# Channel mixers of a two-layer encoder: up and down projections in 2x2 blocks with seven block products, the down projection as a stage of its own with its input by way of DRAM

## The chip, the cores and the metric

The kernel runs on one core of one Trainium2 chip. The metric is the device time of one execution in microseconds. The core's engines work from queues of their own: TensorE (PE, with its weight load PEld), VectorE (DVE), ScalarE (ACT), GpSimd (POOL) and SyncE (SP), which issues most of the transfers between DRAM and on-chip memory.

## What is computed

An encoder of two layers on 1280 tokens: a prompt of 256 and a sample of 1024. Layer 0 mixes tokens by RWKV-7, layer 1 by neighbourhood attention. After each mixer follow its output projection, the residual and a squared-ReLU network of width 4096 on 1024 features, with the same weights for prompt and sample:

```
def _sq_relu_mlp(h, w_up, w_down):
    return jnp.square(jax.nn.relu(h @ w_up)) @ w_down
...
x = x + mixer(_rms_norm(x, norm_mix_g[layer])) @ w_o
x = x + _sq_relu_mlp(_rms_norm(x, norm_mlp_g[layer]), w_up[layer], w_down[layer])
```

(The last two lines are put in short; the mixers' own formulas play no part here.)

## The kernel before

Features lie on the 128 partitions, tokens along the free dimension. The tokens are three segments: s0 is the prompt (256), s1 and s2 are the halves of the sample (512 each). Every matmul operand is split into a high part (a cast to fp32r) and a low part (what the cast left), and every product is three matmuls, high by high, high by low, low by high (`mm3`, L95, issued at L97, L98 and L99). A weight block of 128x1024 is loaded by SP, cast by ACT (L91), and its low part is a subtraction on POOL (L92).

`channel_layer` (L1322) does all that follows a mixer. First comes the **output projection**: for 8 blocks m of output features and three segments, 8 feature blocks k times three matmuls into one PSUM tile `ps` (24 matmuls). DVE adds the tile to the residual stream `x` (L1382), ACT and POOL form sums of squares (L1213, L1214), and `split_x` cuts x, times the norm's gain, into the next operands `ah`, `al` (L1221 on ACT, L1222 on DVE). The root mean square is not applied here: since the squared ReLU is homogeneous of degree two, `scale` (L1388) multiplies the residual x by the mean square ms (L1395, DVE and POOL in turns), and at the very end x is multiplied by its reciprocal (L1399, L1432).

Then come the **up and down projections, interleaved** for 32 blocks f of 128 hidden features: `up(f, s)` (L1401) is 24 matmuls, a ReLU on ACT (L1408), the square on POOL (L1409), the cast on ACT (L1411) and the low part on DVE (L1412). `down([f - 1], s)` (L1418) has 8 output blocks of three matmuls, each added to x by DVE (L1430):

```
for f in range(2, NF - 1):
    for s in range(3):
        up(f, s)
        down([f - 1], s)
    if rest and f > 4:
        inverse(*rest.pop())
    wdown(f)
```

Hidden activations therefore never leave the chip. The last two f go through one `down`, which also scales x, stores it and, in layer 0, splits it for the next layer (L1432 to L1434), sums its squares and takes the token norms; ten `v_block`s (L494, 24 matmuls of 256 columns) of the attention's value projection follow. The order of the instructions on every engine is a scheduler's, except on PE in that last piece. Seven PSUM tiles take turns.

## Time and profile before

| | us |
|---|---|
| median of 3 runs (lowest, highest) | 4359.28 (4358.39, 4360.66) |
| profiled execution, its own time | 4355.5 |
| its span, from the first instruction to the last | 4353.7 |
| mean granted TensorE clock | 0.951 |
| layer 0: output projection to the last v_block | 1648.6 to 2707.1 |
| layer 1: output projection to the end | 3334.9 to 4353.7 |

Times in the rows of the trace are counted from the span's start. Rows by stage or by line give busy time, the number of instructions and, by line, the mean duration in ns; then the idle time of the engine just before them and what ended it. A matmul's recorded duration overlaps its neighbours', so the cost of a matmul on PE is the distance between two starts. PEclk is the granted clock as a share of full speed.

### The profile page before, as it was taken

To read this page: it belongs to the slowest core of one execution; us is meant where nothing else is said; L and a number is where in the kernel's file an instruction comes from. 1 tells how busy PE (TensorE), PEld (TensorE's weight loads), DVE (VectorE), ACT (ScalarE), POOL (GpSimd) and SP (SyncE) were. 2 spreads that over 40 slices of the span, in tenths; PEclk is the share of its full clock that TensorE was granted. 3 is DMA by queue.
4 is the path that set the end of the run, shared out by engine and by line. 5 is a ranking of instruction groups with operands and counts; after the bars stand their busy time and mean duration, and the time that the engine had idled before them with its cause. 6 is when DMAs were issued, how large, how long until landed. Compare 5 with 4: busy or idle time off the path is not lost.

```text
span 4353.7 us, 69827 instructions
## 1 busy us (share of the span) xinstructions
PE 4048.0 (93%) x25060; PEld 3369.9 (77%) x25060; DVE 2695.7 (62%) x5276; ACT 1782.1 (41%) x4705; POOL 1672.1 (38%) x1706
## 2 busy tenths in 40 slices
PE   7888989789999879999999998989998999999999
PEld 4664669778777768888888888977776888888888
DVE  7888874477778755755555556156656665555555
ACT  6764442477777763211111114255545311111111
POOL 5446663234444443422222224134435432222222
PEclk8996779899999989999999999999998999999999
DMA  3234455665666424111111113433334211111111
GB/s 119 82 107 171 162 172 166 153 159 144 158 153 153 112 84 157 49 39 38 36 39 39 39 35 118 147 67 74 76 81 147 77 39 39 35 39 35 39 39 59
DMA packets 484155, 400.27 MB, mean 92 GB/s; under 512 B 289152, under 2 KB 392480, under 8 KB 483808
## 3 DMA queue, kind: packets, MB, share of 16 engines
q1 hardware_dynamic: 447584, 328.56, 27.2%
q10 hardware_dynamic: 34416, 61.35, 3.9%
q0 software_dynamic: 1808, 5.90, 0.4%
q8 instruction: 197, 3.23, 0.3%
q14 instruction: 150, 1.23, 0.1%
HBM read 285.66 MB, written 121.24 MB: 93 GB/s over the span
## 4 chain that ended last, share of the span: by engine, by line
PE 66%; DVE 6%; ACT 5%; DMA 3%; issue 2%; POOL 2%; SPq 1%; ACTq 0%; DVEq 0%; POOLq 0%
PE ps L97 16%; PE ps L99 16%; PE ps L98 16%; PE w L1057 2%; PE us L1029 2%; PE kps L950 1%; PE aps L809 1%; PE vps L501 1%; PE vps L502 1%; PE vps L503 1%; PE us L1043 1%; PE op L1873 1%; PE w L1009 1%; ACT u L1038 1%; PE pt L1815 1%
## 5 line engine op out<-in xcount | busy, mean ns | idle before, releaser
L1430 DVE TENSOR_TENSOR x<-ps,x 128x256 f32<-128x256 f32 x1488 | 814.7, 597 | 627.9 <-PE ps L99 627.7
L97 PE MATMUL ps<-ah,whi 128*128 128x512 f32 (+1 forms) x2304 | 844.2, 366 | 4.2 <-ACT whi L91 3.5
L98 PE MATMUL ps<-al,whi 128*128 128x512 f32 (+1 forms) x2304 | 824.6, 358 | 2.6 <-POOL al L1320 2.6
L99 PE MATMUL ps<-ah,wlo 128*128 128x512 f32 (+1 forms) x2304 | 824.7, 358 | 1.8 <-POOL wlo L92 1.5
L92 POOL TENSOR_TENSOR wlo<-raw,whi 128x1024 fp32r<-128x1024 f32 (+1 forms) x178 | 391.1, 2197 | 850.2 <-ACT whi L91 807.4
L97 PE MATMUL ps<-hh,whi 128*128 128x512 f32 (+1 forms) x1536 | 546.7, 356 | 13.9 <-DVE x L1430 13.9
L99 PE MATMUL ps<-hh,wlo 128*128 128x512 f32 (+1 forms) x1536 | 546.0, 355 | 0.0
L98 PE MATMUL ps<-hl,whi 128*128 128x512 f32 (+1 forms) x1536 | 545.3, 355 | 0.0
L97 PEld LDWEIGHTS ps<-ah,whi 128*128 128x128 f32 x2304 | 439.5, 191 | 78.9 <-issue 12.9
L99 PEld LDWEIGHTS ps<-ah,wlo 128*128 128x128 f32 x2304 | 438.7, 190 | 67.8 <-POOL wlo L92 2.7
L98 PEld LDWEIGHTS ps<-al,whi 128*128 128x128 f32 x2304 | 439.5, 191 | 63.0 <-POOL al L1320 3.0
L91 ACT CAST whi<-raw 128x1024 fp32r<-128x1024 f32 (+1 forms) x206 | 200.8, 975 | 699.2 <-PE ps L98 632.9
L1409 POOL TENSOR_TENSOR rl<-rl 128x512 f32<-128x512 f32 (+1 forms) x192 | 174.2, 907 | 500.5 <-PE ps L99 458.3
L97 PEld LDWEIGHTS ps<-hh,whi 128*128 128x128 f32 x1536 | 291.5, 190 | 57.5 <-DVE x L1430 16.9
L1408 ACT ACTIVATE rl<-ps 128x512 f32<-128x512 f32 (+1 forms) x192 | 100.8, 525 | 546.4 <-PE ps L99 546.4
L99 PEld LDWEIGHTS ps<-hh,wlo 128*128 128x128 f32 x1536 | 291.5, 190 | 41.1
L98 PEld LDWEIGHTS ps<-hl,whi 128*128 128x128 f32 x1536 | 291.3, 190 | 40.9
L1411 ACT CAST hh<-rl 128x512 fp32r<-128x512 f32 (+1 forms) x192 | 105.5, 549 | 320.9 <-POOL rl L1409 320.9
L1051 DVE SCALAR_TENSOR_TENSOR S<-us,dall,sd 64x64 f32<-64x64 f32 x512 | 145.0, 283 | 125.1 <-PE us L1043 113.3
L1013 POOL TENSOR_TENSOR sd<-S,dall 128x128 f32<-128x128 f32 x256 | 122.4, 479 | 256.0 <-DVE S L1051 173.2
L1412 DVE TENSOR_TENSOR hl<-rl,hh 128x512 fp32r<-128x512 f32 (+1 forms) x192 | 119.4, 622 | 151.6 <-ACT hh L1411 151.2
L1057 PE MATMUL w<-u,zb 128*128 128x128 f32 x640 | 158.4, 330 | 47.0 <-ACT u L1038 45.3
(311 smaller groups left out, 8548.8 us busy)
## 6 DMA issues: line engine op xcount, KB each, us to landing
raw<-in_w_down_dram SPq DMA_DIRECT2D x64, 512.0 KB, 3.5
raw<-in_w_up_dram SPq DMA_DIRECT2D x64, 512.0 KB, 3.5
ar<-ar_d SPq DMA_DIRECT2D x80, 256.0 KB, 3.3
bk<-bk_d SPq DMA_DIRECT2D x80, 256.0 KB, 3.6
ar_d<-ar ACTq DMA_DIRECT2D x32, 512.0 KB, 2.7
bk_d<-bk ACTq DMA_DIRECT2D x32, 512.0 KB, 3.5
bs<-tab SPq DMA_DIRECT2D x128, 96.0 KB, 3.7
v_d<-vt ACTq DMA_DIRECT2D x80, 128.0 KB, 4.0
```

The lines of the kernel that those rows point to most:

```text
L91: nc.scalar.copy(hi[:, cs], raw)
L92: lo_eng.tensor_tensor(out=lo[:, cs], in0=raw, in1=hi[:, cs].bitcast(F32), op=ALU.subtract)
L97: mm(ps, sh, mh, start=first, stop=False)
L98: mm(ps, sh, ml, start=False, stop=False)
L99: mm(ps, sl, mh, start=False, stop=last)
L1013: nc.gpsimd.tensor_tensor(out=R["sd"], in0=st["S"], in1=self.dall[:, m, d, ch:ch + 1].to_broadcast([P, P]), op=ALU.mult)
L1051: nc.vector.scalar_tensor_tensor(out=S2[es, es], in0=sn[es, es], scalar=D, in1=R["sd"][es, es], op0=ALU.mult, op1=ALU.add)
L1057: nc.tensor.matmul(w, J["zb"][d, g][:, c, :], R["u2"], start=False, stop=True, skip_group_check=True)
L1409: nc.gpsimd.tensor_tensor(out=r[:, :n], in0=r[:, :n], in1=r[:, :n], op=ALU.mult)
L1411: nc.scalar.copy(hh[:, :n], r[:, :n])
L1412: nc.vector.tensor_tensor(out=hl[:, :n], in0=r[:, :n], in1=hh[:, :n].bitcast(F32), op=ALU.subtract)
L1430: nc.vector.tensor_tensor(out=xv, in0=ps[:, :n], in1=xv, op=ALU.add)
```

## The change

Both products become 2x2 block products with seven block multiplications in the place of eight. `channel_layer` now calls `up_stage` (L1353), then `down_stage` (L1628).

**Up.** The sample's tokens form the two block columns (s1, s2), the 1024 input features the two inner blocks, and a pair p of hidden blocks the two block rows. Sums t1 to t4 of the activations are formed once per layer (`sums`, L1426, beside the output projection, cut at L1381 and after), sums s1 to s4 of the weights once per pair (`up_sums`, L1535). `up_pair` then has seven products of 12 matmuls of 512 columns. Their results are combined by DVE, squared on DVE (one instruction for ReLU and square, L1591), combined again into the seven combinations that the down projection needs (four subtractions, two on DVE, two on POOL), and stored to DRAM (`hv_d`). The prompt is done as before (`up_s0`, 24 matmuls of 256), its square stored to `hs_d`. The residual x is stored to `xo_d`, the mean squares and their reciprocals to `ms_d`.

**Down.** Four groups g of 1024 hidden features, each with eight steps i: a block of the weights (a11 to a22 are the four blocks, s1 to s4 sums of them) times one of the seven stored combinations (4 output blocks of 12 matmuls of 512 columns), or, with the four plain blocks, times the prompt (4 times 12 matmuls of 256). While a step's products run, the next step's operands are made in four quarters (`prep`, L1699): a weight sum on DVE (L1712 to L1718), its cast on ACT and low part on POOL, the cast of the loaded activations on ACT and their low part on DVE (`cut`, L1695 to L1697). Loaded activations go through a ring of five tiles `hr`. `evict` adds the products to the outputs, on DVE from PSUM and on POOL from on-chip tiles (all of them at L1734). The residual comes in on POOL in groups 1 and 2 (table `CALM`, L1838 and L1839); scaling, storing and squares in group 3 (`finish`, L1756). In this stage the order on all five engines is the order of the code.

The diff, cut to its core (`scale` loses its multiplications of x; what else is removed is the code of `up` and `down` above):

```diff
+            with self.tc.manual_schedule(engines={mybir.EngineType.PE}):
+                if gate:
+                    up.enter_context(self.clctx)
+                self.up_stage(up, layer, x_src, wname, gate)
+                up.close()
+                self.actctx.close()
+            E = mybir.EngineType
+            with self.tc.manual_schedule(engines={E.PE, E.DVE, E.Activation, E.Pool, E.SP}):
+                self.down_stage(layer, dst, gnext)
...
+            nc.vector.tensor_tensor(out=xv, in0=ps[:, :n], in1=xv, op=ALU.add)
+            nc.sync.dma_start(xo_d[m, :, c0:c1], xv)
...
+        def sums(k):
+            x1, x2, y1, y2 = x[1][:, k], x[2][:, k], x[1][:, k + 4], x[2][:, k + 4]
+            t1, t3, t2, t4 = (ev(k % 2) for _ in range(4))
+            nc.scalar.activation(t1, x1, AF.Copy, scale=g(k))
+            nc.vector.scalar_tensor_tensor(out=t1, in0=x2, scalar=g(k), in1=t1, op0=ALU.mult, op1=ALU.subtract)
+            nc.scalar.activation(t3, x2, AF.Copy, scale=g(k))
+            nc.vector.scalar_tensor_tensor(out=t2, in0=y2, scalar=g(k + 4), in1=t1, op0=ALU.mult, op1=ALU.subtract)
+            nc.vector.scalar_tensor_tensor(out=t3, in0=y2, scalar=g(k + 4), in1=t3, op0=ALU.mult, op1=ALU.subtract)
+            nc.vector.scalar_tensor_tensor(out=t4, in0=y1, scalar=g(k + 4), in1=t2, op0=ALU.mult, op1=ALU.subtract)
...
-            def scale(s):
-                c0, c1 = SEGS[s]
-                n = c1 - c0
-                ps = pn.tile([P, 512], F32, name="nps", tag="nps")
-                nc.tensor.matmul(ps[:, :n], ones, ms[s], start=True, stop=True)
-                nc.vector.tensor_scalar(out=ms[s], in0=ps[:, :n], scalar1=1.0 / (KT * P), scalar2=RMS_EPS, op0=ALU.mult, op1=ALU.add)
-                for m in range(8):
-                    (nc.gpsimd if m % 2 else nc.vector).tensor_tensor(out=x[s][:, m], in0=x[s][:, m], in1=ms[s], op=ALU.mult)
...
+        W0 = self.up_weights(layer, 0, wp)
+        self.up_s0(wk, 0, W0, hs_d)
+        scale(2)
...
+            cut(var["t2", k], kept[k]["t2"], e[k % 2])
...
+        for p in range(16):
+            W = W0 if p == 0 else self.up_weights(layer, p, wp)
+            self.up_sums(W, st, sp)
+            if 0 < p < 15:
+                self.up_s0(wk, p, W, hs_d, (0, 1) if p < 14 else (0,))
+            if p < 15:
+                self.up_raw[p + 1] = self.up_load(layer, p + 1, wp)
+            waiting, self.stores = self.stores, []
+            self.up_pair(p, W, B, lambda: ev(p % 2 == 1), hv_d)
...
+        nc.vector.tensor_tensor(out=s1, in0=r1[:, lo], in1=r1[:, hi], op=add)
+        s2 = st()
+        nc.vector.tensor_tensor(out=s2, in0=s1, in1=r0[:, lo], op=sub)
+        cut("s2", s2, nc.gpsimd)
+        s3 = st()
+        nc.gpsimd.tensor_tensor(out=s3, in0=r0[:, lo], in1=r1[:, lo], op=sub)
+        cut("s3", s3, nc.vector)
+        cut("s1", s1, nc.gpsimd)
+        s4 = st()
+        nc.vector.tensor_tensor(out=s4, in0=r0[:, hi], in1=s2, op=sub)
+        cut("s4", s4, nc.vector)
...
+        def prod(w, b):
+            ps = self.pm.tile([P, 512], F32, name="ps", tag="ps")
+            for k in range(4):
+                ks = slice(k * P, k * P + P)
+                self.mm3(ps, W[w][0][:, ks], W[w][1][:, ks], *B[b][k], k == 0, k == 3)
+            return ps
...
+        ps = prod(("a", 0, 0), "b11")
+        nc.scalar.copy(a, ps)
+        ps = prod("s2", "t2")
+        plus(c, ps, a)
+        ps = prod(("a", 0, 1), "b21")
+        plus(a, ps, a)
+        square(a)
+        store(0, a)
+        ps = prod("s3", "t3")
+        plus(e, ps, c)
+        p5 = prod("s1", "t1")
+        plus(c, p5, c)
+        ps = prod(("a", 1, 1), "t4")
+        plus(d, ps, e)
+        square(d)
+        store(3, d)
+        plus(e, p5, e)
+        square(e)
+        store(6, e)
+        ps = prod("s4", "b22")
+        plus(c, ps, c)
+        square(c)
+        self.store()
+        nc.vector.tensor_tensor(out=a, in0=c, in1=a, op=sub)
+        store(4, a)
+        nc.gpsimd.tensor_tensor(out=c, in0=e, in1=c, op=sub)
+        store(1, c)
+        nc.vector.tensor_tensor(out=e, in0=e, in1=a, op=sub)
+        store(2, e)
+        nc.gpsimd.tensor_tensor(out=d, in0=d, in1=e, op=sub)
+        store(5, d)
...
+        STEPS = [("a21", 0, None), ("a11", 1, 0), ("s3", 7, 1), ("s2", 6, 2), ("s1", 5, 4), ("a12", 2, 3), ("a22", 4, 5), ("s4", 3, 6)]
+        CALM = {1: [(0, 4), (0, 5), (2, 0), (2, 1)], 5: [(1, 4), (1, 5)], 6: [(1, 0), (1, 1), (2, 4), (2, 5)], 7: [(0, 0), (0, 1)]}
...
+            while loads and len(staged) <= ahead:
+                src = loads.pop(0)
+                t = hr()[:, :src.shape[-1]]
+                nc.sync.dma_start(t, src)
+                staged.append(t)
...
+        def cut(d, t, eng):
+            nc.scalar.copy(d[0], t)
+            eng.tensor_tensor(out=d[1], in0=t, in1=d[0].bitcast(F32), op=sub)
...
+            def quarter(k):
+                tt = vec.tensor_tensor
+                r = lambda b: R[b][k]
+                if n == "s3":
+                    tt(out=r("a11"), in0=r("a11"), in1=r("a21"), op=sub)
+                elif n == "s2":
+                    tt(out=r("a11"), in0=r("a22"), in1=r("a11"), op=sub)
+                elif n == "s1":
+                    tt(out=r("a21"), in0=r("a21"), in1=r("a22"), op=add)
+                elif n == "s4":
+                    tt(out=r("a11"), in0=r("a12"), in1=r("a11"), op=sub)
+                cut(W[k], r({"s3": "a11", "s2": "a11", "s1": "a21", "s4": "a11"}.get(n, n)), pool)
+                if H:
+                    cut(H[k], fetch(), vec)
+                if i in (0, 5):
+                    cut(Z[i == 5][k], fetch(), vec)
...
+            if q == 1:
+                nc.scalar.copy(u[m], ps)
+            if q == 6:
+                plus(vec, u[m], ps, u[m])
+                plus(pool, o22, o22, u[m])
+            if q == 5:
+                plus(pool, o21, o21, u[m])
+            if q == 2 and g:
+                plus(pool, o12, o12, u[m])
+            for o in {1: (o11,), 7: (o21, o22), 5: (o22, o12), 2: (o11,), 4: (o21,), 3: (o12,)}.get(q, ()):
+                if g == 0 and q in (1, 7):
+                    nc.scalar.copy(o, ps)
+                elif g == 0 and q == 5 and o is o12:
+                    plus(vec, o, ps, u[m])
+                else:
+                    plus(vec, o, ps, o)
...
+            vec.tensor_tensor(out=M[s][m], in0=M[s][m], in1=inv[s], op=mul)
+            late.append((dst[m, :, c0:c1], M[s][m]))
...
+                if s not in begun:
+                    begun.add(s)
+                    nc.scalar.activation(accs[s], M[s][m], AF.Square)
+                else:
+                    sq = rp.tile([P, 512], F32, name="sq", tag="sq", bufs=2)[:, :n]
+                    nc.scalar.activation(sq, M[s][m], AF.Square)
+                    pool.tensor_tensor(out=accs[s], in0=accs[s], in1=sq, op=add)
...
+            quarters = ((0, 1), (2,), (3,), ())
+            for m in range(4) if H else ():
+                ms = slice(P * m, P * m + P)
+                for k in quarters[m] if n != "s4" or g < 3 else (m,):
+                    quarter(k)
+                ps = pm.tile([P, 512], F32, name="ps", tag="ps")
+                for k in range(4):
+                    self.mm3(ps, W[k][0][:, ms], W[k][1][:, ms], *H[k], k == 0, k == 3)
+                evict(g, q, m, ps)
...
+                t = xs.pop((s, m))
+                pool.tensor_tensor(out=t, in0=t, in1=inv[s], op=mul)
+                pool.tensor_tensor(out=M[s][m], in0=M[s][m], in1=t, op=add)
...
+        for n, (g, i) in enumerate(order):
+            W, H, _ = ready
...
+            products(g, i, W, H, quarter)
```

**The order of instructions.** On PE, 18003 rows become 17235.

First place, DVE between the output projection's last eviction and the first products of the up projection, layer 0. Before (x2 is the residual's third segment, al its low parts, ms0 and x0 the scaling of the prompt, hl the low part of hidden activations):

```order
L1382 TENSOR_TENSOR x2_18550<-ps_19354,x2_18550 128x512
L1222 SCALAR_TENSOR_TENSOR al6_18291<-x2_18550,vec_62,ah6_18290 128x512
L1222 SCALAR_TENSOR_TENSOR al7_18293<-x2_18550,vec_62,ah7_18292 128x512
L1393 TENSOR_SCALAR ms0_18559<-nps_19437 128x256
L1395 TENSOR_TENSOR x0_18548<-x0_18548,ms0_18559 128x256
L1412 TENSOR_TENSOR hl_19434<-rl_19430,hh_19433 128x256
```

After (ev and st are tiles with sums of activations and of weights, raw the weights as loaded, t2l3 the low part of the fourth tile of t2):

```order
L1417 TENSOR_TENSOR x2_18603<-ps_19493,x2_18603 128x512
L1228 SCALAR_TENSOR_TENSOR al6_2_18324<-x2_18603,vec_62,ah6_2_18323 128x512
L1433 SCALAR_TENSOR_TENSOR ev_19525<-x2_18603,vec_62,ev_19523 128x512
L1434 SCALAR_TENSOR_TENSOR ev_19524<-x2_18603,vec_62,ev_19524 128x512
L1435 SCALAR_TENSOR_TENSOR ev_19526<-x1_18602,vec_62,ev_19525 128x512
L1228 SCALAR_TENSOR_TENSOR al7_2_18326<-x2_18603,vec_62,ah7_2_18325 128x512
L1469 SCALAR_TENSOR_TENSOR st_19541<-x2_18603,vec_62,st_19541 128x512
L1469 SCALAR_TENSOR_TENSOR st_19546<-x2_18603,vec_62,st_19546 128x512
L1403 TENSOR_SCALAR ms2_18606<-nps_19621 128x512
L1407 RECIPROCAL st_19625<-ms2_18606 128x128 x4
L1547 TENSOR_TENSOR st_19666<-raw_19552 128x512
L1549 TENSOR_TENSOR st_19668<-st_19666,raw_19551 128x512
```

Two low parts stood between the last eviction and the scaling; now there are also five sums, the mean square with four reciprocals and the first weight sums.

Second place, DVE in the projections' steady part. Before, in the f loop of layer 0 (ps a product, x1 the residual):

```order
L1430 TENSOR_TENSOR x1_18549<-ps_20791,x1_18549 128x512
L1430 TENSOR_TENSOR x1_18549<-ps_20796,x1_18549 128x512
L1412 TENSOR_TENSOR hl_20788<-rl_20784,hh_20787 128x512
L1430 TENSOR_TENSOR x1_18549<-ps_20801,x1_18549 128x512
L1430 TENSOR_TENSOR x1_18549<-ps_20806,x1_18549 128x512
```

After, in step i = 2 of a group of the down stage (a11 and a22 raw weight blocks, v1l the low part of the loaded activations hr, o21 and o22 outputs):

```order
L1714 TENSOR_TENSOR a11_24077<-a22_24181,a11_24077 128x512
L1697 TENSOR_TENSOR v1l_24448<-hr_24282,v1h_24447 128x512
L1714 TENSOR_TENSOR a11_24078<-a22_24182,a11_24078 128x512
L1697 TENSOR_TENSOR v1l_24450<-hr_24294,v1h_24449 128x512
L1734 TENSOR_TENSOR o21_0_23077<-ps_24469,o21_0_23077 128x512
L1734 TENSOR_TENSOR o22_0_23076<-ps_24469,o22_0_23076 128x512
L1714 TENSOR_TENSOR a11_24079<-a22_24183,a11_24079 128x512
L1697 TENSOR_TENSOR v1l_24452<-hr_24317,v1h_24451 128x512
L1734 TENSOR_TENSOR o21_1_23081<-ps_24491,o21_1_23081 128x512
L1734 TENSOR_TENSOR o22_1_23080<-ps_24491,o22_1_23080 128x512
```

The evictions of the running step now alternate with weight sums and low parts for the next one.

Third place, POOL. Before, in the f loop (rl the squared activations, wlo the low part of a weight block):

```order
L1409 TENSOR_TENSOR rl_21399<-rl_21399 128x256
L1409 TENSOR_TENSOR rl_21471<-rl_21471 128x512
L92 TENSOR_TENSOR wlo_21827<-raw_21828,whi_21826 128x1024
L1409 TENSOR_TENSOR rl_21543<-rl_21543 128x512
L92 TENSOR_TENSOR wlo_21821<-raw_21822,whi_21820 128x1024
```

After, in steps i = 3 and 4 of group 1 (w0l and w1l low parts of the next weights, u0 to u3 a product shared by three outputs):

```order
L1697 TENSOR_TENSOR w0l_24548<-a21_23753,w0h_24547 128x512
L1697 TENSOR_TENSOR w0l_24550<-a21_23754,w0h_24549 128x512
L1734 TENSOR_TENSOR o22_0_23076<-o22_0_23076,u0_23091 128x512
L1697 TENSOR_TENSOR w0l_24552<-a21_23755,w0h_24551 128x512
L1734 TENSOR_TENSOR o22_1_23080<-o22_1_23080,u1_23094 128x512
L1697 TENSOR_TENSOR w0l_24554<-a21_23756,w0h_24553 128x512
L1734 TENSOR_TENSOR o22_2_23084<-o22_2_23084,u2_23097 128x512
```

Squares are gone from POOL here; low parts of 512 columns and additions of two on-chip tiles have come in.

512 lines of the change are left out of this document (369 added, 143 removed).

## The prediction, made before the run

> **What bounds the kernel now.** I read the page's first part, then the stages one by one: for each stretch busy time and instructions of PE, PEld, DVE, ACT and POOL, the granted clock, the share of the DMA engines, GB/s.
>
> ```profile
> PE 4048.0 (93%) x25060; PEld 3369.9 (77%) x25060; DVE 2695.7 (62%) x5276; ACT 1782.1 (41%) x4705; POOL 1672.1 (38%) x1706
> PE 66%; DVE 6%; ACT 5%; DMA 3%; issue 2%; POOL 2%; SPq 1%; ACTq 0%; DVEq 0%; POOLq 0%
> ```
>
> ```profile
> 1648.60:1758.80 110.20, 107.55 (x556) 92.68 (x557) 48.07 (x68) 40.77 (x62) 37.80 (x27) 0.98 0.41 138
> 1758.80:1841.50 82.70, 78.32 (x388) 65.74 (x387) 66.47 (x88) 20.54 (x34) 43.45 (x29) 0.98 0.11 34
> 1841.50:2612.60 771.10, 771.10 (x4034) 665.76 (x4033) 410.98 (x757) 146.44 (x224) 209.16 (x140) 1.00 0.11 39
> 2612.60:2707.10 94.50, 82.77 (x505) 74.48 (x503) 62.11 (x97) 39.00 (x80) 46.56 (x35) 0.93 0.34 102
> 3445.10:3527.40 82.30, 78.16 (x384) 64.83 (x383) 66.06 (x87) 19.41 (x33) 42.76 (x29) 0.98 0.11 34
> 3527.40:4307.20 779.80, 779.80 (x4033) 666.59 (x4032) 412.54 (x759) 145.53 (x223) 206.90 (x139) 1.00 0.11 37
> 4307.20:4353.70 46.50, 41.86 (x218) 35.52 (x216) 26.31 (x45) 4.28 (x7) 15.73 (x13) 1.00 0.31 113
> ```
>
> PE is the bound where the change works. In the third and sixth stretch (28 of 32 blocks f each) it is busy without a gap at full clock, while DVE is at 53%, POOL at 27%, DMA at 11%. Every matmul less is time won there, until something else becomes late. The stretches around them have gaps.
>
> What a matmul costs is the distance of starts in PE's timeline; between these two lie 24 matmuls:
>
> ```profile
> 1907.87 0.39 PE L97 MATMUL ps<-hh,whi 128*128 128x512 f32 x1
> 1913.31 0.39 PE L97 MATMUL ps<-ah,whi 128*128 128x512 f32 x1
> ```
>
> So 5.44 / 24 = 0.2267 us for 512 columns. One f has 96 of these, 21.76 us, and 48 of 256 columns; 771.1 / 28 = 27.54 leaves 5.78, or 0.12 each.
>
> **What the change removes.** Sum 1, matmuls. Up and down had 32 x 27.54 = 881.3 us per layer. A pair now has 84 of 512 and 48 of 256 columns: 19.04 + 5.76 = 24.8; 16 pairs are 396.8. A down group has 336 and 192, 99.2; four are 396.8. Together 793.7: **-87.6** in layer 0. Layer 1 runs at 779.8 / 28 = 27.85 for the same work, so **-88.6**. Sum -176.
>
> Sum 2, gaps that go with the old code. The second stretch holds three up and two down, 5 x 13.77 = 68.8, in 82.7: 13.9 lost; layer 1 in 82.3: 13.5. Layer 0's last stretch holds three halves of an f, 41.3, and 240 v_block matmuls, 28.8: 24.4 of its 94.5 lost; layer 1's end loses 46.5 - 41.3 = 5.2. Sum **-57**. What is late in their place is counted next.
>
> **What it adds.** The up pairs themselves I cost at nothing: matmuls of 24.8 us cover, by durations below, some 12 us of DVE and 12 of POOL, and weights are loaded a pair ahead. If that cover is gone, each us per pair costs 32. Durations by form, layer 0:
>
> ```profile
> L92 POOL TENSOR_TENSOR wlo<-raw,whi 128x512 fp32r<-128x512 f32 x14 | 18.2, 1298 | 27.9 <-ACT whi L91 27.9
> L1409 POOL TENSOR_TENSOR rl<-rl 128x512 f32<-128x512 f32 x64 | 66.9, 1046 | 240.4 <-PE ps L99 231.1 <-ACT rl L1408 9.3
> L1412 DVE TENSOR_TENSOR hl<-rl,hh 128x512 fp32r<-128x512 f32 x64 | 45.1, 705 | 63.0 <-ACT hh L1411 62.8
> L1411 ACT CAST hh<-rl 128x512 fp32r<-128x512 f32 x64 | 39.8, 621 | 133.6 <-POOL rl L1409 133.5
> L1222 DVE SCALAR_TENSOR_TENSOR al<-x,vec,ah 128x512 fp32r<-128x512 f32 x16 | 17.5, 1144 | 1.5 <-ACT ah L1221 1.5
> L1214 POOL TENSOR_TENSOR ms<-ms,sq 128x512 f32<-128x512 f32 x14 | 24.7, 1762 | 60.5 <-ACT sq L1213 60.5
> L1399 DVE RECIPROCAL ms<-ms 128x128 f32<-128x128 f32 x10 | 8.8, 923 | 0.3
> ```
>
> *Up's start.* After the last projection PE has the prompt (48 x 0.12) and one product (12 x 0.2267): 8.5 us of cover. The next product needs s2 and t2. Ahead of t2's last low part DVE has seven operations like L1222's (8.0), the mean square, four reciprocals (3.7) and two weight sums: some 14.5, and the copies on ACT and POOL's additions delay it to about 16.5. That is 8 lost, 2 more at the next products, and 2 for a slow clock (below): 12 per layer, bounds 4 (DVE runs ahead) and 18. **+24**.
>
> *Down, the chain of quarters.* This is the largest term. A quarter with a weight sum is a chain over three engines: sum on DVE (0.69, the first row of the next fence), cast of weights on ACT (0.62), cast of activations on ACT (0.62), low part on DVE (0.69); DVE's queue is in order, so the next quarter's sum stands behind this low part. That is 2.62. Beside it POOL makes the weights' low part. Two timelines, DVE and POOL, show what then happens:
>
> ```profile
> 4348.46 0.69 DVE L1432 TENSOR_TENSOR x<-x,ms 128x512 f32<-128x512 f32 x1
> ```
>
> ```profile
> 2627.84 2.42 DVE L1432 TENSOR_TENSOR x<-x,ms 128x256 f32<-128x256 f32 x1
> 2630.18 0.41 DVE L1430 TENSOR_TENSOR x<-ps,x 128x256 f32<-128x256 f32 x1
> ```
>
> ```profile
> 2627.57 2.41 POOL L92 TENSOR_TENSOR wlo<-raw,whi 128x1024 fp32r<-128x1024 f32 x1 [4.63 <-ACT whi L91]
> 2629.92 1.24 POOL L1409 TENSOR_TENSOR rl<-rl 128x512 f32<-128x512 f32 x1
> ```
>
> A DVE operation on two on-chip tiles ended with POOL's (2.42 us for 256 columns), one with its input from PSUM did not wait (0.41). The Trainium skill ("SBUF — State Buffer", Who interferes with whom) says that DVE with two SBUF inputs and GpSimd share a port pair that one of them holds for a whole instruction, and that a DVE operation with one SBUF input is free of it; the trace agrees, 2.42 against 0.41. By that rule the hold below is certain; without it the sum would keep 2.62 per quarter.
>
> So a low part on POOL (1.05 to 1.30 by the rows; I take 1.1) starts at 1.31 of the quarter and holds DVE's from 1.93 to 2.41: the quarter takes **3.1**. In steps i = 2, 3, 4 PE has only 10.9 us each (48 x 0.2267). While i = 2 runs: four quarters, 12.4, two evictions of two additions (2.7) between them on DVE, less 2.3, since the last quarter is needed three quarters into the next first product: 12.8. While i = 3 runs: 12.4, two evictions of one (1.4), two of POOL's additions (1.3 each) that hold the port, the last low part (1.1): 17.5. While i = 4 runs, without sums: 4 x 1.93, two evictions of two (2.7), three POOL additions (3.9): 14.3. Together 44.6 against 32.7, 11.9 lost per group, 95 over eight; the other steps have 16.6 us of PE and hide theirs. Bounds: 2 per group without a hold (16 in all), 17 with every hold doubled (136). I take **+95**, since the row of 2.42 us is the case in question.
>
> *Residual* on POOL in groups 1 and 2: 16 operations of 512 and 8 of 256, 26 us more on POOL beside its 57 (44 x 1.3), and 34 of two-tile work on DVE: 117 us in a group of 111. Bounds 0 and 21 (four groups at 5); I take 4 each, **+16**.
>
> *Clock.* PE's timeline in layer 0's old last stretch:
>
> ```profile
> 2656.22 0.40 PE L99 MATMUL ps<-hh,wlo 128*128 128x512 f32 x1
> 2659.70 0.49 PE L97 MATMUL ps<-hh,whi 128*128 128x512 f32 x1 [3.09 <-DVE x L1430]
> ...
> 2660.63 0.63 PE L97 MATMUL ps<-hh,whi 128*128 128x512 f32 x1
> 2661.05 0.63 PE L98 MATMUL ps<-hl,whi 128*128 128x512 f32 x1
> ```
>
> After 3.09 us idle the pitch is 0.42, half speed; such a gap costs some 2 us more. The chain above opens gaps of 2 to 6 us: one slow start per group, **+16**; bounds 0 and 32. The Trainium skill ("TensorE: Matmul & The Clock Gate", Part 1) puts the limit at an idle window of about 3.4 us; here 3.09 was enough, and at 3.4 this term would be nearer 8.
>
> *Group 3's finish.* Sixteen multiplications on DVE, 11 us, in layer 0 also fourteen additions of squares on POOL like L1214's (1.76): 14 in layer 0 (5 to 26), 4 in layer 1 (0 to 8). **+18**.
>
> *Ends*: v_blocks wait for the last splits and norms, 8 (4 to 20), and layer 1's tail 5, as now. **+13**. *Output projection's start*: its tiles come from pools opened later; no row shows it; 0 to 10 per layer, I take 5. **+10**.
>
> Stores and loads by DRAM: 7 + 2 half-size results out per pair, about 2 MB, with 1 MB of weights in 24.8 us is some 125 GB/s, below the 138 of the first stretch, and the ring of five tiles asks about a step ahead. The page has
>
> ```profile
> raw<-in_w_up_dram SPq DMA_DIRECT2D x64, 512.0 KB, 3.5
> ```
>
> so 3.5 us to landing against some 11: nothing.
>
> Added: 24 + 95 + 16 + 16 + 18 + 13 + 10 = 192. On the profiled execution, 4355.5 - 176 - 57 + 192 = 4314.5. It lay 3.8 below the median of the runs shown (4359.28), so 4318 as a median.
>
> **Rivals.** *A, PE stays the bound in the down groups*: ACT and DVE work far enough ahead (POOL's low part then starts late enough not to hold DVE), and the chain costs 16, no slow clock, 8 for the residual. Then 79 + 16 + 8 = 103 less: **4215**. For it: DVE had 47% idle in the steady part. Against it: two tiles per operand only, so no quarter can start before the step before last has ended.
>
> *B, the port sets the pace (slower)*: every two-tile DVE operation in the quarters pays what it paid beside POOL in the old scaling of layer 0,
>
> ```profile
> L1395 DVE TENSOR_TENSOR x<-x,ms 128x512 f32<-128x512 f32 x8 | 12.1, 1563 | 0.0
> ```
>
> 1.56 for 0.69. A quarter is then 1.56 + 0.62 + 0.62 + 1.56 = 4.36 where I have 3.1; over the eight quarters with sums in steps 2 and 3 that is 10.1 per group, 81 in all: **4399**. It decides from a quarter of 3.1 + 41 / 64 = 3.74 on. For it: POOL has 44 to 68 such operations per group. Against it: in L1395's stretch both engines had nothing else in line, here they wait for ACT in between.
>
> *C, the way by DRAM is late*: if stores of up and loads of down collide so that a landing takes more than a step, 11 us against 3.5, each of 28 steps waits; at 2 us it is +56, 4374. That the change doesn't save what it says is excluded: 768 fewer instructions stand on PE.
>
> **How the numbers follow.** Forecast 0.50, A 0.27, B 0.20, C 0.03. Predicted is 4318. The range runs from 4190 (A with its smaller terms at their low bounds) to 4400 (B); the forecast's own is 4260 to 4370. A measurement tells 0.2%, 8.7 us, from no change. Faster by more: A and 0.42 of the forecast, 0.69. Within: 0.07, the upper part of the forecast and B's lower edge. Slower: most of B, C and the forecast's tail, 0.24.
>
> **What would show it.** Groups of the down stage near 111 us, not 99, with PE waiting in steps 3 and 4 for DVE's or POOL's low parts: right; without these waits A. Pairs of the up stage at 24.8 with full clock; if they are longer, the cover that I counted is missing. DVE's weight sums near 0.7 and low parts near 1.2: the hold as I have it; both near 1.5: B. An idle PE of some 8 us in layer 0's first pair: the start. Wrong would be my sum if PE waits for transfers, or if groups 1 and 2 are more than 5 us longer than group 0.

## The result and the profile after

The changed kernel takes **4375.7 us** (median of 5 runs, 4373.6 to 4379.5) where the kernel before took 4358.4 beside it: a ratio of **1.0047, interval 1.0032 to 1.0061**. It is slower by 17 us. The forecast was 4318, faster by 0.9%; the time lies in the range given, near rival B, but on the other side of no change. The profiled execution took 4379.5, 3.8 above the median.

The page after, its first lines (compare 93% PE, 62% DVE, 38% POOL before):

```profile
span 4377.8 us, 70379 instructions
PE 3966.5 (91%) x24292; PEld 3270.3 (75%) x24292; DVE 2936.7 (67%) x4954; ACT 1981.6 (45%) x5143; POOL 2290.1 (52%) x2126
```

The matmuls are gone as planned (768 fewer), and the kernel is longer. To see where the time went, I cut both executions at the same five events: the end of layer 0's output projection, the end of its tenth value block, the last product of attention, the end of layer 1's output projection, and the end. Busy time of PE, PEld, DVE, ACT, POOL, granted clock, DMA share and GB/s, first before:

```profile
0.00:1758.80 1758.80, 1532.48 (x11052) 1241.12 (x11053) 1260.47 (x2530) 1044.07 (x3211) 823.54 (x1021) 0.90 0.50 140
1758.80:2706.20 947.40, 931.44 (x4918) 805.42 (x4917) 539.52 (x939) 205.21 (x336) 299.17 (x204) 0.99 0.14 45
2706.20:3337.00 630.80, 576.15 (x3909) 464.65 (x3907) 345.45 (x858) 325.07 (x840) 252.60 (x279) 0.95 0.37 96
3337.00:3445.10 108.10, 108.10 (x561) 91.79 (x558) 45.30 (x62) 38.53 (x58) 31.40 (x22) 1.00 0.38 131
3445.10:4353.70 908.60, 899.81 (x4631) 766.94 (x4629) 504.92 (x889) 169.23 (x262) 265.39 (x181) 1.00 0.12 41
```

and after:

```profile
0.00:1759.50 1759.50, 1537.80 (x11077) 1243.93 (x11078) 1275.64 (x2532) 1052.62 (x3229) 862.11 (x1041) 0.90 0.50 143
1759.50:2711.60 952.10, 887.96 (x4507) 749.23 (x4506) 639.20 (x774) 295.37 (x538) 567.08 (x396) 0.95 0.36 123
2711.60:3358.20 646.60, 583.17 (x3911) 471.66 (x3910) 349.92 (x861) 325.85 (x840) 252.16 (x279) 0.94 0.38 94
3358.20:3480.60 122.40, 116.54 (x578) 98.40 (x579) 55.50 (x63) 48.09 (x74) 71.40 (x41) 0.96 0.47 159
3480.60:4377.80 897.20, 841.08 (x4227) 707.06 (x4225) 616.43 (x727) 259.66 (x464) 537.37 (x371) 0.96 0.37 126
```

| stretch | before | after | difference | by the forecast's terms |
|---|---|---|---|---|
| to the end of layer 0's output projection | 1758.8 | 1759.5 | +0.7 | +5 |
| layer 0, up, down and the first ten value blocks | 947.4 | 952.1 | +4.7 | -28.4 |
| rest of the value blocks, attention | 630.8 | 646.6 | +15.8 | 0 |
| layer 1, output projection | 108.1 | 122.4 | +14.3 | +5 |
| layer 1, up, down, end | 908.6 | 897.2 | -11.4 | -22.8 |
| sum | 4353.7 | 4377.8 | +24.1 | -41.2 |

The channel mixers together (second and fifth row) gained 6.7 us instead of 51, and the stretches between them lost 30 instead of 5. The second and fifth stretch have POOL and DVE busy for far longer and a granted clock of 0.95 and 0.96 where it was 0.99 and 1.00. Cut further, up and down of layer 0, then of layer 1:

```profile
1759.50:2181.10 421.60, 408.29 (x2115) 346.49 (x2113) 259.81 (x307) 99.38 (x159) 228.36 (x152) 0.98 0.33 119
2181.10:2663.60 482.50, 437.86 (x2114) 362.81 (x2114) 353.04 (x413) 172.49 (x331) 330.05 (x239) 0.93 0.40 130
3480.60:3901.10 420.50, 408.34 (x2115) 346.50 (x2113) 263.17 (x307) 98.92 (x159) 228.61 (x152) 0.99 0.33 119
3901.10:4377.80 476.70, 432.75 (x2112) 360.55 (x2112) 353.27 (x420) 160.75 (x306) 308.75 (x220) 0.94 0.40 132
```

Matmuls alone are 396.8 in each of the four. So up loses 25 and 24 us, down 86 and 80, 5 of these in the tail. Part of it is slow clock: a mean of 0.93 over 482.5 us and of 0.94 over 476.7 withholds 34 and 29 us of full speed. That is an upper bound, since some of it falls into PE's waits.

Most of the rest stands in PE's waits in layer 0's down stage, 46 us in all (engine and tile, what it waited for; us, times, the longest):

```profile
PE ps L99 <- ACT v1h L1696: 11.8, 7, 3.7
PE ps L101 <- POOL w0l L1697: 7.2, 8, 1.6
PE ps L100 <- DVE v1l L1697: 6.1, 8, 1.2
PE ps L99 <- ACT v0h L1696: 5.7, 3, 2.3
```

and why, in DVE's and ACT's timelines of a step i = 3 in which the weights' sums of the next are made:

```profile
2336.54 0.68 DVE L1716 TENSOR_TENSOR a<-a,a 128x512 f32<-128x512 f32 x1
2338.50 1.35 DVE L1697 TENSOR_TENSOR v0l<-hr,v0h 128x512 fp32r<-128x512 f32 x1 [1.28 <-ACT v0h L1696]
2339.78 0.68 DVE L1716 TENSOR_TENSOR a<-a,a 128x512 f32<-128x512 f32 x1
```

```profile
2337.33 0.62 ACT L1696 CAST w0h<-a 128x512 fp32r<-128x512 f32 x1 [4.48 <-DVE a L1716]
2337.86 0.61 ACT L1696 CAST v0h<-hr 128x512 fp32r<-128x512 f32 x1
2340.57 0.62 ACT L1696 CAST w0h<-a 128x512 fp32r<-128x512 f32 x1 [2.10 <-DVE a L1716]
```

This is the chain of the prediction, term by term: sum, cast, cast, low part, next sum. From sum to sum are 3.24 us; 3.1 was forecast. ACT waits for a weight sum and only then casts the activations, for which it does not wait; DVE waits 1.28 us for that cast, and its low part takes 1.35 instead of 0.68 beside POOL's (1.28 us, from 2338.03). Over the stage DVE's low parts take 1.34 to 1.40 us in the mean, POOL's 1.42 to 1.48.

### The profile page after: what moved, and what is told of

It reads as the page before. It is cut to its first block, busy times and chain, and to the rows that moved or that the text cites. A ratio compares the mean times of both kernels' runs of the same rounds, so it can differ in the third digit from the quotient of the medians.

```text
span 4377.8 us, 70379 instructions
## 1 busy us (share of the span) xinstructions
PE 3966.5 (91%) x24292; PEld 3270.3 (75%) x24292; DVE 2936.7 (67%) x4954; ACT 1981.6 (45%) x5143; POOL 2290.1 (52%) x2126
## 5 line engine op out<-in xcount | busy, mean ns | idle before, releaser
L99 PE MATMUL ps<-ah,whi 128*128 128x256 f32 (+1 forms) x1536 | 545.6, 355 | 7.8 <-ACT whi L93 7.8
L101 PE MATMUL ps<-ah,wlo 128*128 128x256 f32 (+1 forms) x1536 | 525.8, 342 | 3.2 <-POOL wlo L94 3.2
L100 PE MATMUL ps<-al,whi 128*128 128x256 f32 (+1 forms) x1536 | 525.4, 342 | 0.0
L1588 DVE TENSOR_TENSOR ev<-ps,ev 128x512 f32<-128x512 f32 x224 | 153.9, 687 | 183.4 <-PE ps L101 178.5
L1528 POOL TENSOR_TENSOR wlo<-raw,whi 128x1024 fp32r<-128x1024 f32 x64 | 172.3, 2692 | 187.1 <-ACT whi L1527 184.1
L1697 POOL TENSOR_TENSOR w1l<-a,w1h 128x512 fp32r<-128x512 f32 x128 | 187.8, 1479 | 139.5 <-ACT w1h L1696 103.0
L1015 POOL TENSOR_TENSOR sd<-S,dall 128x128 f32<-128x128 f32 x256 | 122.4, 479 | 256.1 <-DVE S L1053 169.8
L1697 POOL TENSOR_TENSOR w0l<-a,w0h 128x512 fp32r<-128x512 f32 x128 | 180.7, 1422 | 121.0 <-ACT w0h L1696 114.3
L94 POOL TENSOR_TENSOR wlo<-raw,whi 128x1024 fp32r<-128x1024 f32 (+1 forms) x76 | 145.1, 1910 | 178.3 <-ACT whi L93 178.1
L1697 DVE TENSOR_TENSOR v0l<-hr,v0h 128x512 fp32r<-128x512 f32 x112 | 157.2, 1410 | 90.6 <-ACT v0h L1696 90.6
L1697 DVE TENSOR_TENSOR v1l<-hr,v1h 128x512 fp32r<-128x512 f32 x112 | 151.8, 1361 | 90.4 <-ACT v1h L1696 90.4
```

Of the source, the lines that this page charges most:

```text
L94: lo_eng.tensor_tensor(out=lo[:, cs], in0=raw, in1=hi[:, cs].bitcast(F32), op=ALU.subtract)
L99: mm(ps, sh, mh, start=first, stop=False)
L100: mm(ps, sh, ml, start=False, stop=False)
L101: mm(ps, sl, mh, start=False, stop=last)
L1015: nc.gpsimd.tensor_tensor(out=R["sd"], in0=st["S"], in1=self.dall[:, m, d, ch:ch + 1].to_broadcast([P, P]), op=ALU.mult)
L1528: nc.gpsimd.tensor_tensor(out=lo, in0=raw, in1=hi.bitcast(F32), op=ALU.subtract)
```

## Experiments

My theory after the profile: the down stage is bound by the serial chain of a quarter (*chain*); first rival: by the time in which DVE's and POOL's two-tile work excludes each other (*port*). Beside them stand the costs that the forecast had not counted.

### The order of the two casts, and who makes the low parts

`a2_h_first` changes the order of two calls in `quarter`:

```diff
-                cut(W[k], r({"s3": "a11", "s2": "a11", "s1": "a21", "s4": "a11"}.get(n, n)), pool)
                 if H:
                     cut(H[k], fetch(), vec)
+                cut(W[k], r({"s3": "a11", "s2": "a11", "s1": "a21", "s4": "a11"}.get(n, n)), pool)
```

> The changed kernel, in each quarter of the down stage the loaded activations are cut ahead of the weights: on ACT the cast of the activations stands before that of the weights, on DVE the low part follows the weight sum without the second cast in between. Chain theory (three engines in series set the pace): a quarter loses one cast, 0.6 us, of its chain, steps 2 to 4 get 6 to 9 us shorter per group, groups fall from 118-123 to about 111, some 60 us less in all, 4315. Port theory (two-tile work of DVE and POOL excludes each other): the same operations hold the same port, groups stay within 3 us, 4365 to 4385.

Measured: **4286.3 us, 0.983 of before (0.9812 to 0.9848)**, 89 less than the changed kernel. (The expectation counted a group from its second step; whole stages are compared here. The gain is half as much again as the 60 us that it named.) Down takes, layer 0, then layer 1 with its end:

```profile
2186.40:2620.90 434.50, 413.37 (x2114) 347.18 (x2114) 350.66 (x413) 172.91 (x331) 342.66 (x239) 0.98 0.46 145
3856.20:4284.70 428.50, 408.71 (x2112) 345.64 (x2112) 348.88 (x420) 161.13 (x306) 321.65 (x220) 0.99 0.46 147
```

48 us less in each, with the same work on DVE (351 for 353) and more on POOL. The clock rose from 0.93 to 0.98 and from 0.94 to 0.99: what it withholds falls from 34 and 29 us to 9 and 4, so up to about half of the 96 us is full speed regained. Steps 2, 3 and 4, where the prediction had put the chain, took 175 us in layer 0's four groups and now take 133 (matmuls alone: 131). DVE's timeline of the same step no longer waits for ACT:

```profile
2329.37 0.67 DVE L1716 TENSOR_TENSOR a<-a,a 128x512 f32<-128x512 f32 x1
2329.97 0.68 DVE L1697 TENSOR_TENSOR v0l<-hr,v0h 128x512 fp32r<-128x512 f32 x1
2330.57 0.68 DVE L1716 TENSOR_TENSOR a<-a,a 128x512 f32<-128x512 f32 x1
2331.30 1.64 DVE L1697 TENSOR_TENSOR v0l<-hr,v0h 128x512 fp32r<-128x512 f32 x1
```

The chain theory holds; the port theory, by which the same operations take the same time, falls. What PE still waits for in layer 0's down stage is POOL, the engine that is now the later one:

```profile
PE ps L101 <- POOL w1l L1697: 9.6, 13, 1.6
PE ps L99 <- ACT w1h L1696: 3.2, 2, 2.8
PE ps L99 <- DVE o L1734: 3.0, 1, 3.0
```

`a3_wlo_dve` leaves the order as it was and takes the weights' low parts from POOL.

```diff
-                cut(W[k], r({"s3": "a11", "s2": "a11", "s1": "a21", "s4": "a11"}.get(n, n)), pool)
+                cut(W[k], r({"s3": "a11", "s2": "a11", "s1": "a21", "s4": "a11"}.get(n, n)), vec)
```

> The changed kernel, the low part of the weights in the down stage made by DVE instead of POOL; the order within a quarter stays. Port theory: POOL's holds go (its additions stay), DVE's low parts fall from 1.37 to 0.7 us, groups fall to 105-110 although DVE has 32 operations of 0.7 us more per group: 40 to 60 us less, 4315 to 4335. Chain theory: the chain of a quarter keeps its two casts and gains an operation on DVE in place of a hold; groups stay at 117 to 122, the time within 15 us of 4376.

Measured: 4351.4 us, 0.9985 (0.9973 to 0.9997), 24 less than the changed kernel: between the two. Down fell from 482.5 to 464.2 in layer 0, and DVE's low parts of activations from 1.37 to 0.96 us, not to 0.7, since POOL's additions stayed. So the port costs some 15 to 18 us per layer as long as the chain is there, net of the 32 operations per group that DVE took over; both are real, and the chain is the larger.

With the activations first, `c2_half_wlo` gave every second low part of the weights to DVE and `c3_all_wlo` all of them; both hold the placement of `a1_pad128` (below) too.

```diff
-.get(n, n)), pool)
+.get(n, n)), vec if k % 2 else pool)
```

> As a2_h_first and a1_pad128 together, and in the down stage the low parts of every second quarter's weights made by DVE instead of POOL. Additive: 4286 - 15 = 4271 without the third edit. Port theory (in the groups with the residual POOL's load sets the pace once the chain is short: groups 2 and 3 have 107.8 and 117.5 in layer 0, group 1 101.7): 16 of 32 operations leave POOL, groups 2 and 3 fall by 5 to 8 us each, about 4245. Rival (DVE's longer list delays its own evictions): groups get longer by 2 to 5 us, 4290.

> As c2_half_wlo, with all low parts of the weights made by DVE. Port theory: POOL keeps only additions, groups 2 and 3 fall to 102 like group 1, about 4240. DVE then has some 88 us of work in groups of 101: if its queue sets the pace, groups 0 and 1 rise above 102, 4260 to 4280.

Measured: 4293.7 us, 0.9848 (0.9831 to 0.9865), and 4292.7, 0.9842 (0.9824 to 0.986), against 4271 for the first two edits added up. Port theory's forecasts were missed by 50 us; the rival of the first (4290) came out, the second lies 13 above its rival's 4280. Once the chain is short, DVE's in-order list of sums, low parts and evictions is what is late (PE's largest wait in `c2_half_wlo` is for DVE's `v0l`, 8.2 us in layer 0's down stage), and POOL is the better place.

### The residual

`a6_no_residual` leaves out the residual's work on POOL in groups 1 and 2, but for one pair of operations, so its outputs lack the residual.

```diff
-                pool.tensor_tensor(out=t, in0=t, in1=inv[s], op=mul)
-                pool.tensor_tensor(out=M[s][m], in0=M[s][m], in1=t, op=add)
+                if (s, m) == (0, 0):
+                    pool.tensor_tensor(out=t, in0=t, in1=inv[s], op=mul)
+                    pool.tensor_tensor(out=M[s][m], in0=M[s][m], in1=t, op=add)
```

> The changed kernel without the residual's multiplications and additions on POOL in groups 1 and 2, but for one pair; the outputs lack the residual. By the prediction's term 4 us per group go, 16 in all: 4360. If POOL's port time sets the pace in these groups, they fall to group 0's length (112 us where group 2 has 121), up to 20 us; if the steps that hold the residual have time to spare, nothing changes, 4376.

Measured: one execution, 4340.8 us (4362.7 before, beside it). Down takes 461.8 and 453.4 (to its last product; 482.5 and 471.4 with the residual):

```profile
2177.30:2639.10 461.80, 427.29 (x2112) 356.21 (x2112) 337.16 (x412) 170.87 (x327) 269.11 (x191) 0.94 0.42 136
3880.50:4333.90 453.40, 425.06 (x2112) 355.64 (x2112) 338.72 (x418) 160.37 (x306) 249.27 (x174) 0.95 0.42 137
```

20.7 and 18.0 us: **39 in all, where the forecast had 16 and an upper bound of 21**. The term failed in size and in place: the length of group 1 fell by 2 us only, that of groups 2 and 3 by 7 to 10 each. POOL's queue of the changed kernel where group 1 ends, and PE's first wait in group 2, show why:

```profile
2405.93 1.29 POOL L1839 TENSOR_TENSOR o<-o,xr 128x512 f32<-128x512 f32 x1
2407.18 5.85 POOL L1697 TENSOR_TENSOR w0l<-a,w0h 128x512 fp32r<-128x512 f32 x4
```

```profile
2408.50 0.39 PE L101 MATMUL ps<-z0h,w0l 128*128 128x256 f32 x1 [1.39 <-POOL w0l L1697]
```

Eight operations of the residual in a row (from 2395.7 on) stand ahead of the four low parts that the next group's first step needs. That step is the prompt's product alone, 48 x 0.12 = 5.8 us of matmuls. It took 13.0 us in group 2 and 12.6 in group 3, but 5.7 in both without the residual; in layer 1 12.9 and 11.9 became 5.8. These four steps are 27 of the 39 us.

### The pitch of matmuls

In the up stage the pairs lie 25.26 us apart, not 24.8, without a wait. PE's timeline after, twelve matmuls from the first row to the second:

```profile
1834.56 0.40 PE L99 MATMUL ps<-t2h,sh 128*128 128x512 f32 x1
...
1837.35 0.39 PE L99 MATMUL ps<-ah,whi 128*128 128x512 f32 x1
```

2.79 / 12 = 0.2325 us at full granted clock; the forecast took 0.2267 from layer 0 before. In the built program the left-hand tiles (`t2h`, `ah`, `v0h`, `w0h`) lie at addresses that end in 0xc0, the right-hand ones (`sh`, `whi`) at 0x40. `a1_pad128` makes one tile at the right-hand end 128 bytes longer, which moves these right-hand tiles to 0xc0:

```diff
-        self.tn = cr.tile([P, 40], F32, name="tn")
+        self.tn = cr.tile([P, 72], F32, name="tn")
```

> The changed kernel with one tile of the right-hand memory made 128 bytes longer, so that every right-hand tile starts at an address with the low byte of the left-hand ones (0xc0); nothing else moves. Placement theory: a matmul of 512 columns costs 0.227 us when its two operands agree in that low byte and 0.233 when they don't, so the up pairs fall from 25.3 to 24.8 us in both layers, layer 1's down groups get 2 to 4 us shorter (its mixed steps 11.3 become 11.1), layer 0's down steps with mixed tiles stay (there the tiles then lie at 0x80), attention gains some us too; in all 20 to 30 us less than the changed kernel, about 4350. Traffic theory (the pitch follows the DRAM traffic, 124 GB/s for 39 before): pairs stay at 25.3 and the time at 4375.

Measured: **4360.9 us, 1.0006 (0.9995 to 1.0016)**, 15 less than the changed kernel. Twelve matmuls of an `s1` product:

```profile
1899.76 0.39 PE L99 MATMUL ps<-ah,sh 128*128 128x512 f32 x1
...
1902.48 0.28 PE L99 MATMUL ps<-ah,whi 128*128 128x256 f32 x1
```

2.72 / 12 = 0.2267, and the pairs lie 24.82 apart in both layers. The traffic is the same (121 GB/s for 119), as the up stage of layer 0 shows:

```profile
1762.00:2176.90 414.90, 402.19 (x2115) 346.85 (x2113) 260.30 (x307) 98.72 (x158) 230.66 (x152) 0.98 0.34 121
```

There is a control in it: the down stage's second pair of operand tiles (`v1h`, `w1h`) came to lie at 0x80 in layer 0 and at 0xc0 in layer 1. Layer 1's steps of 48 matmuls with one operand from each side fell from 11.13 to 10.91 us, from start to start. Layer 0's still take 11.0 to 11.2, and its steps with both operands at 0x80 take 10.9. So it is not one good address: the low bytes of the two operands' addresses have to agree. Traffic is ruled out. Two parts of the expectation failed. From the end of layer 0's down stage to the last product of attention are 693 us, 695 without the edit; and of layer 1's down groups only the first got 2 us shorter, the others less than 1, as would be where the chain and not PE sets the pace. So it was 15 us in all for the 20 to 30 expected.

### The seams

Five kernels asked why PE waits where stages meet. SP after, in layer 1's output projection, and ACT among the value blocks of attention, each with what it waited for:

```profile
3356.76 13.89 SPq L1393 DMA_DIRECT2D x<-x_d  x24
3371.04 0.97 SPq L1418 DMA_DIRECT2D xo_d<-x  x2
3372.32 0.33 SPq L92 DMA_DIRECT2D raw<-in_w_no_dram  x1
```

```profile
2721.93 0.62 ACT L93 CAST whi<-raw 128x512 fp32r<-128x512 f32 x1 [5.56 <-DMA raw<-in_w_nk_dram]
2737.71 0.62 ACT L93 CAST whi<-raw 128x512 fp32r<-128x512 f32 x1 [6.26 <-DMA raw<-in_w_nq_dram]
2747.28 0.47 ACT L509 ACTIVATE vt<-vps,tn 128x256 f32<-128x256 f32 x1 [8.58 <-DMA bpm<-tab]
```

The residual's 24 loads occupy SP for 14 us, with the weights of layer 1's output projection behind them. `a4_weights_first` put one weight block ahead of them, `a7_xo_by_act` moved the stores that follow to ACT's queue:

```diff
+        todo = [a[wname][m] for m in ORDER[len(wo):] + ORDER]
+        weights(todo.pop(0))
         for s, ms_ in ((0, range(8)), (1, range(8)), (2, range(8))):
             xload(s, ms_)
-        todo = [a[wname][m] for m in ORDER[len(wo):] + ORDER]
```

```diff
-            nc.sync.dma_start(xo_d[m, :, c0:c1], xv)
...
+            nc.scalar.dma_start(xo_d[m, :, c0:c1], xv)
```

> The changed kernel, the third weight block of the output projection loaded ahead of the 24 loads of the residual instead of behind them on SP. Queue theory: PE's waits for weights in layer 1's output projection (4.2 and 1.6 us, and about 3 us of slow clock behind them) go, 6 to 10 us less, about 4368; layer 0 the same. Rival (the loads wait for memory that attention holds until its end): the waits stay, 4376.

> The changed kernel with the residual's stores in the output projection issued by ACT, behind the square, instead of by SP. Queue theory (loads of weights stand behind stores that wait for PE): the waits of 3 to 4 us for a weight block's cast in layer 1's output projection go, its length falls from 122 to about 113 us, total about 4367. Rival (the weight ring of two raw tiles is the limit): the waits stay.

Measured: 4385.6 us, 1.0058 (1.004 to 1.0076), and 4389.1 in one execution. In the first the waits moved on to a later block (3.0 and 1.9 us), in the second the wait for weights grew to 8.6. Neither one block ahead nor stores elsewhere help; the 24 loads still hold SP, for 13.2 and 18.6 us. `c1_seams`, on `a2_h_first`, loads the residual as the kernel before did, several blocks to a transfer and the last segment late, and makes the first pair's weight sums earlier:

```diff
-            for m in ms_:
-                nc.sync.dma_start(x[s][:, m], x_src[m, :, c0:c1])
+            k0, k1 = ms_[0], ms_[-1] + 1
+            nc.sync.dma_start(x[s][:, k0:k1], x_src[k0:k1, :, c0:c1].rearrange("k p t -> p k t"))
...
+                if seg == (0, 1) and i in (3, 5):
+                    xload(2, range(4) if i == 3 else range(4, 8))
...
             cut(var["t2", k], kept[k]["t2"], e[k % 2])
+        self.up_sums(W0, st, sp)
```

> As a2_h_first, with two seams changed: the residual is loaded by five transfers instead of 24, those of the third segment only after the fourth and sixth weight block; and the weight sums of the first up pair stand ahead of the cuts of t3 and t4. Issue theory (SP spends 13 us in a row on 24 residual loads, the weights stand behind them): layer 1's output projection loses its 3 to 5 us waits for weight casts and falls from 122 to about 114 us. Start theory (POOL's and DVE's queues hold s2 back): the waits of 6.9 and 3.8 us before the second product fall by about 3 together in each layer. Both: some 14 us less than a2_h_first, 4272. If both are wrong: 4286.

Measured: 4283.4 us, 0.9815 (0.9796 to 0.9835); beside `a2_h_first` the intervals overlap, so the time does not show a gain. Its trace shows what changed, though of its fastest execution (4272.4; the other three took 4281.3 to 4285.7). No wait for weights is left on PE in layer 1's output projection:

```profile
PE op L2292 <- DVE ot L2293: 1.5, 1, 1.5
PE nps L1402 <- POOL ms L1424: 1.4, 1, 1.4
PE pt L2234 <- ACT s L2235: 0.5, 1, 0.5
```

and from attention's last product to the first pair's second product are 131.2 us, 140.5 in `a2_h_first`. SP now issues three loads ahead of the weights, where 24 took 13.89 us:

```profile
3306.75 2.85 SPq L1393 DMA_DIRECT2D x<-x_d  x3
```

So the residual's loads in front of the weights were the cause there. The edit changed their number and the place of the last two together; which of the two counts is not shown. At up's start the wait of 3.8 us for POOL's `sl` went, the wait of 6.9 for ACT's `sh` stayed. `a5_reciprocals_late` had taken four reciprocals out of DVE's list there, to group 3 of the down stage:

```diff
+            if s == 2:
+                return
             inv = st()[:, :c1 - c0]
...
+                for c in range(0, 512, P):
+                    vec.reciprocal(out=inv[2][:, c:c + P], in_=inv[2][:, c:c + P])
```

> The changed kernel with the four reciprocals of the last segment's mean squares taken out of the start of the up projection; they are made on DVE in the down stage, at the start of group 3. Theory of the prediction (DVE's list ahead of the first sums is what PE waits for): PE's wait of 6.9 us for the cast of s2 falls by about 3.7, with less slow clock behind it, 4 to 6 us less per layer, about 4366. Rival (the wait is for POOL's low parts or the weights): the wait before the second product stays near 7 us.

Measured: one execution, 4384.9 us, where 4366 was expected. The first wait fell from 6.9 to 6.0, the second rose from 3.8 to 5.4. In layer 1 the waits went from 6.9 and 2.6 to 6.0 and 5.4. The reciprocals that the prediction counted are not what sets the start: without them DVE's next sum waits for POOL.

```profile
1772.79 1.08 DVE L1551 TENSOR_TENSOR st<-st,raw 128x512 f32<-128x512 f32 x1 [1.78 <-POOL al L1381]
```

DVE's list and POOL's end close together here, and taking something from one of them moves the wait.

`a8_outputs_on_top` opens the pool of the down stage's outputs first, so that the place of attention's first weight tile is free earlier.

```diff
+        mp = self.lpool(right, "mp", "right")
         vq = self.lpool(right, "vq", "right")
         tp = self.lpool(right, "tp", "right")
-        mp = self.lpool(right, "mp", "right")
```

> The changed kernel with the pool of the down stage's outputs opened first on the right-hand side, ahead of the value weights, so that the place of the attention's first weight tiles comes free after the fourth value block instead of the tenth. Memory theory (the weights of attention are loaded late because their place is held): ACT's waits of 5.6 to 8.6 us for weights among the value blocks go, PE's two waits of 4.4 us with them, 8 to 14 us less between the end of layer 0's down stage and the attention's first statistics, about 4365. Rival (the loads are late for another reason, an order on SP or ACT): nothing changes.

Measured: one execution, 4377.7 us. PE's two waits for `vt` went (8.4 us together, the longer 4.4); waits for value weights (3.2 and 2.1 us) and for the norms (3.3) came in their place, and from the end of the down stage to attention's last product are 692.4 us, for 694.6. The memory held by the down stage explains those two waits, not the 15.8 us of this stretch. The stretch's granted clock was 0.94 for 0.95, which withholds at most some 7 us more. **What else lengthens it stays open.**

### Together

`d1_all_three` joins the edits of `a2_h_first`, `a1_pad128` and `c1_seams`.

> The changed kernel with the three edits that helped: activations cut first (a2_h_first), equal low bytes of addresses (a1_pad128), the residual's loads in five transfers and the first pair's weight sums earlier (c1_seams). Additive theory: 4376 - 89 - 15 - 5 = 4267. If the placement and the chain cost the same time (a shorter chain makes PE the bound in the down groups, so that the faster matmuls count in full there), up to 8 us less, 4259; if the edits hide behind one another, 4283 as c1_seams.

Measured: **4253.0 us (4248.9 to 4264.3), 0.9754 of before (0.9734 to 0.9774)**, 2.5% faster than the kernel before and 2.8% faster than the changed one. This is 14 us below the three edits added up and 6 below the lowest of the expected times. The change's seven products do pay once the order around them is right: 108 us net, where the matmuls alone save 176. The comparison favours the change a little: the kernel before has the slower pitch in layer 1 too (27.85 us per f for 27.54), and it was not given the padding.

## Why the prediction was wrong

- **The matmuls saved** (-176): right in number. 0.2267 us per matmul of 512 columns was measured with tiles at other addresses; here 0.2325. Up's sixteen pairs took 16 x 25.26 = 404 per layer, 7 more than forecast in layer 0 and 3 in layer 1, where 27.85 per f already held part of it. The edit that aligns the tiles gave 15 us.
- **The chain of quarters** (+95): right as a mechanism; the swap of `a2_h_first` shows it. A quarter took 3.24 us for 3.1; layer 0's steps 2, 3 and 4 of group 1 took 10.9, 18.8 and 17.1 us, 47 in all, for 44.6. Over the eight groups these steps lost 90 us, half speed in them included, where chain and clock had 95 + 16. The prediction read the chain from the code and then took it as given; that one swap of two calls takes it apart it did not see.
- **The residual** (+16, bounds 0 and 21): failed. 39. I had compared POOL's and DVE's time with the group's length and called the excess the cost, and had written that the other steps "have 16.6 us of PE and hide theirs". A group's last step has 10.9 and its first only 5.8, and the first waits for low parts that stand behind the residual's work on POOL. The prediction had named the sign: groups 1 and 2 more than 5 us longer than group 0. Group 2 was 8.5 and 9.5 us longer (120.9 for 112.4, 121.6 for 112.1).
- **Clock** (+16, bounds 0 and 32): mis-sized. The granted clock of the down stage was 0.93 and 0.94, up to 34 and 29 us withheld. One slow start costs more than the 2 us assumed (after the gap of 3.09 us in the old kernel the clock stayed at 0.50 for 6.8 us), and there were two or three per group, not one. How much of it comes on top of the chain is not told apart: the edit that removed the waits brought 0.98 and 0.99 with it. With chain and finish these terms were 129 in the forecast; down's losses without the residual are about 122 (86 + 80, less the tail's 5 and the residual's 39). That the stage as a whole came out near its forecast is in part luck: the residual's 23 us too few were made up by 21 too many in steps 2 to 4.
- **Up's start** (+24): 31. From the end of the output projection to the second pair's second product are 49.8 and 48.7 us, and the 192 matmuls between take 33.8. The sum was near, the reason wrong: it is not DVE's list with its reciprocals alone but POOL's as well.
- **The seams** (value blocks and norms +8, output projections +10, attention nothing): this is the step that failed most. The first ten value blocks took 48.0 us for 36.8, the rest of attention 15.8 more where no term stood at all, and layer 1's output projection 14.3 more for 5. The prediction put attention at nothing and gave no reason; I took the change to lie inside the channel mixers. It also split the residual's loads into 24, the cause of the waits in the projection, and left the down stage's memory held to the end, the cause of two waits. The larger part of the 15.8 stays open; that a scheduler chose another order in code that the diff does not touch is a guess.

Summed, the forecast's span was 4312.5, the measured one 4377.8. Of the 65 us, 21 lie in attention, layer 1's projection and the start (15.8 + 9.3 - 4.3), 11 in the first value blocks, 20 in up (12.8 and 7.3), 11 in down (8.2 and 3.0), and 2 in rounding of the cuts. No single term turned the sign: a gain of 41 was the small difference of 233 and 192, and most terms came out on the dear side. Rival B gave the right sign for the wrong reason, since its condition, a quarter above 3.74 us, was not met.

## What to carry to other kernels

When operands are prepared in a pipeline over several in-order engines, let the branch whose input is already there go first on each of them: here one swap was worth 89 us. When a forecast is the small difference of large sums, price the stretches on both sides of the change too, with the transfers and the memory that it hands over. And measure a matmul's cost with the tiles where they will lie.

## What the runs showed of the hardware

- The pitch of a 512-column fp32r matmul depends on where its two operands lie: 0.2267 us where the low bytes of their addresses agree, 0.2325 where they differ by 128, and 0.229 or 0.2333 (steps of 11.0 and 11.2 us) where they differ by 64. Pairs 25.26 us apart came to lie 24.82 apart with 128 bytes of padding. The kernel before has both pitches too, unremarked: layer 0's f took 27.54 us and layer 1's 27.85.
- Short waits in a row cost clock. Of the 42 waits in layer 0's down stage the longest was 3.7 us and all but five were below 2, yet the granted clock was 0.93; in `a2_h_first`, with 22 us of waits for 46, it was 0.98. The stage's start, PE alone (busy time, granted clock, DMA share and GB/s):

```profile
2179.05:2182.46 3.41, 1.18 (x8) 1.00 0.16 60
2182.47:2189.29 6.82, 5.54 (x20) 0.50 0.74 236
```

  Two waits, of 1.28 and 1.01 us, and then half speed for 6.8 us. Each of the stage's 12 stretches at half speed, 3.4 or 6.8 us long, follows 3.4 us in which PE was idle for 1.5 to 2.7 us in all. The Trainium skill ("TensorE: Matmul & The Clock Gate", A second HAM failure mode) tells of a kernel in which frequent short idles between groups of matmuls make the clock go back and forth; the trace agrees with that, more than with the limit on a single gap that the prediction used.
- A two-tile operation on DVE beside one on POOL took twice its time (1.35 for 0.68 us), as in the profile before, but spreading such work over both engines did not pay once the chain was short.
